# Opening in written order with two value heads together, spectra a value block later, key weights' low halves by adding transfer

## The chip, the cores and the metric

One core of a Trainium2 chip (trn2) runs one launch of the kernel. The metric is the device time of that launch in microseconds (us); lower is better. Engines are named as in the profile: PE (matmuls), PEld (its weight loads), DVE (VectorE), ACT (ScalarE), POOL (GpSimd), SP (the queue from which most transfers are issued).

## What is computed

One layer of a diffusion backbone over 512 latent tokens of width 1024, with 256 context tokens beside them, all in float32. Cut to what matters here:

```python
mod = silu(c) @ w_ada + b_ada          # six vectors of 1024: sh1, sc1, g1, sh2, sc2, g2; the same for c_ctx
hc = rmsnorm(ctx, norm1_g) * (1 + csc1) + csh1
h = rmsnorm(x, norm1_g) * (1 + sc1) + sh1
k, v, gates = h @ w_in[:, :Q_OFF]      # keys, values of four heads, gates; of hc too
q, o, hy, gm, gh = h @ w_in[:, Q_OFF:] # queries, output gate, three Hyena streams, merge gates
y = gm * (mlstm(q, k, v, gates) * o @ w_pm) + gh * (hyena(hy, spectra) @ w_ph)
x = x + g1 * (y @ w_out)
x = x + g2 * swiglu(rmsnorm(x, norm2_g) * (1 + sc2) + sh2)
return rmsnorm(x, final_g)
```

The Hyena spectra come from a small network of three sine layers, a product with its last weights, a decay window and a Fourier transform.

## The kernel before

**Products.** Tokens lie along the columns, features along the 128 partitions, in eight tiles of 128 (KT = 8). A product in float32 accuracy is made of three matmuls (mm3, L234 to L236): every operand is split into a high half rounded to the matmul's type and a low half, and high times high, high times low and low times high are added up. A split (L215, L216) is an ACT copy for the high half and a DVE subtraction for the low one. wsplit loads 512 KB of weights into a tile "wr" and splits them into "wh" and "wl"; each of the three tags has four buffers. gemm runs one output tile: 24 matmuls of 512 columns (or 256 for the context). Those that finish a group are noted in a list, and behind() queues work behind the last noted one on PE.

**Order.** The code is traced once, and a scheduler orders each engine's instructions by priority, which falls in the order written, and by readiness. high_priority(600) lets a block go earlier, issue_after(x) keeps a block behind x. Transfers are issued from SP in the order of that queue, stores from POOL.

**The opening** (from L1032). SP issues: the packed vectors (vecs, 190 KB), a small bias (bgb, 8 KB), the filter network's input (net, 386 KB), the input xT in four pieces of 512 KB, constant matrices (mats, 320 KB), 16 pieces of 256 KB of the modulation's weights for features 0 to 511 (ada_load, L329), and ahead of the last four of those one query weight (512 KB); then the first spectrum's vectors and weights, three query weights, the Fourier tables (dftf, 640 KB), the modulation's other 16 pieces, the context (1 MB). ACT squares the eight input tiles and DVE adds them (sq_sums, L403, L404), PE sums over the partitions (L407), POOL raises to the power -1/2 (L392), PE broadcasts the row to a bank (L394), DVE multiplies four input tiles (L1082). Between these run the stages of the filter network (filter_network, L420 and L423 on PE, L426 to L431 on DVE, a sine on ACT, L433) and ada_first: 32 products (64 matmul records) of 32 columns (L338), an ACT copy (L344), two transposes (L347), four DVE adds and the scale (L354, L355). modulate makes the high half of an input tile on ACT (L1113), the full value on DVE (L1118) and the low half on DVE (L1119), for tiles 0 to 3 once the first half of the modulation is there and for tiles 4 to 7 after the second (modulated). part(i, p) runs half of query tile i, four input tiles, as mm3 in the order of the tiles; the four query tiles stay in four banks. The first spectrum's steps (filter_spectrum: four products L464 and L465 with the window multiplied in on DVE, L466; sums and differences L468 to L470; a split; then 36 matmuls, three ACT copies and four DVE instructions, L503 to L508, and a store) are interleaved with these, all three steps of it.

**After the opening.** v_head (L661 to L673) makes one head's values: six blocks of 128 tokens, four of the latents and two of the context; for head 0 with the gates, one block to a bank (272 columns), for the others two (256 columns); 144 matmuls a head. The loop over the four heads runs v_head, a late query tile (q_late), and next_spectrum, which closes the open spectrum (its 36 matmuls) behind the last noted matmul and opens the next (its eight products and the split). Then eight key tiles (k_tile) run, each one gemm for 512 and one for 256 columns with convolution and SiLU on ACT and DVE and two stores on POOL; after every second one next_spectrum, and at the first of these the gates' arithmetic (gate_math). Further on: the Hyena stage, the mLSTM heads, the output products and the feed-forward layer, which the change leaves alone. There, weight_sums already has an adding transfer from POOL (L1649).

## Time and profile before

| | us |
|---|---|
| three runs, lowest, median, highest | 1200.3, 1203.37, 1204.35 |
| the profiled execution | 1201.67 |
| its span, first to last instruction | 1199.9 |

The profile is of one execution of its own. Engine times are busy times within the span; a row of a timeline gives start, length, engine, line, operation, tile written and tiles read, the count of instructions merged, and in brackets the idle time before it with what ended it.

### The profile page before, as it was taken

What the parts mean: (1) busy time and instruction counts of PE and PEld (TensorE: products, weight loads), DVE (VectorE), ACT (ScalarE), POOL (GpSimd) and SP (SyncE); (2) the same over time, 40 slices, a digit from 0 to 9 for tenths busy, and PEclk for the clock granted to TensorE, in tenths of its full rate; (3) what the DMA queues carried; (4) which work ended last, traced back from release to release, by engine and by line L of the source; (5) the groups of instructions that cost most, each with busy time, mean ns of one, the idle gap of its engine ahead of it and who ended that gap; (6) DMA issues with size and microseconds to landing.
All of it is one profiled execution on the core that took longest, in us unless ns stands there. A gap on an engine that the chain in (4) does not pass through costs nothing.

```text
span 1199.9 us, 18671 instructions
## 1 busy us (share of the span) xinstructions
PE 1166.0 (97%) x7136; PEld 1032.7 (86%) x7136; DVE 936.9 (78%) x1507; ACT 569.1 (47%) x887; POOL 113.8 (9%) x193
## 2 busy tenths in 40 slices
PE   4999999999999999999999999999999999999997
PEld 2799988988888888888788888779999999998886
DVE  5967798987989999899647887685878999896332
ACT  3763465754554455444756543233444544462221
POOL 0011110110000010101131131000101111100000
PEclk9899999999999999999999999999999999999998
DMA  9745443454245342434685586794447777757312
GB/s 346 257 144 175 144 163 117 143 206 142 100 140 184 115 155 91 173 112 137 215 249 177 181 255 220 259 310 160 136 136 185 185 185 181 189 185 250 97 49 70
DMA packets 74217, 207.50 MB, mean 173 GB/s; under 512 B 9736, under 2 KB 13584, under 8 KB 71568
## 3 DMA queue, kind: packets, MB, share of 16 engines
q1 hardware_dynamic: 56720, 154.92, 39.2%
q0 software_dynamic: 17408, 51.39, 14.4%
q8 instruction: 56, 0.92, 0.3%
q14 instruction: 33, 0.27, 0.1%
HBM read 170.62 MB, written 35.65 MB: 172 GB/s over the span
## 4 chain that ended last, share of the span: by engine, by line
PE 87%; DVE 6%; DMA 3%; ACT 2%; issue 1%; POOL 0%; SPq 0%; DVEq 0%; POOLq 0%; ACTq 0%
PE bank L234 25%; PE bank L235 25%; PE bank L236 25%; PE bank L1558 2%; PE bank L661 2%; PE bank L662 2%; PE bank L663 2%; DMA wr<-in_wph 1%; DMA wr<-in_wada 1%; DVE wl L216 1%; PE bank L617 1%; PE bank L464 1%; PE bank L465 1%; DMA ul<-in_xT 1%; PE bank L338 0%
## 5 line engine op out<-in xcount | busy, mean ns | idle before, releaser
L215 ACT ACTIVATE wh<-wr 128x1024 fp32r<-128x1024 f32 (+2 forms) x185 | 190.8, 1033 | 331.2 <-PE bank L235 226.1
L234 PE MATMUL bank<-hTh,wh 128*128 128x512 f32 (+1 forms) x896 | 326.8, 365 | 2.0 <-ACT hTh L1113 2.0
L235 PE MATMUL bank<-hTl,wh 128*128 128x512 f32 (+1 forms) x896 | 325.9, 364 | 1.9 <-DVE hTl L1119 1.9
L236 PE MATMUL bank<-hTh,wl 128*128 128x512 f32 (+1 forms) x896 | 325.4, 363 | 0.0
L216 DVE TENSOR_TENSOR wl<-wr,wh 128x1024 fp32r<-128x1024 f32 (+2 forms) x185 | 219.5, 1190 | 100.7 <-ACT wh L215 99.3
L234 PEld LDWEIGHTS bank<-hTh,wh 128*128 128x128 f32 x896 | 169.9, 190 | 27.0 <-ACT hTh L1113 2.2
L235 PEld LDWEIGHTS bank<-hTl,wh 128*128 128x128 f32 x896 | 169.7, 189 | 26.6 <-DVE hTl L1119 2.4
L236 PEld LDWEIGHTS bank<-hTh,wl 128*128 128x128 f32 x896 | 169.6, 189 | 25.5
L235 PE MATMUL bank<-big,wh 128*128 128x256 f32 (+1 forms) x346 | 110.7, 320 | 1.1 <-DVE big L216 1.1
L234 PE MATMUL bank<-big,wh 128*128 128x256 f32 (+1 forms) x346 | 110.9, 320 | 0.5 <-ACT big L215 0.5
L236 PE MATMUL bank<-big,wl 128*128 128x256 f32 (+1 forms) x346 | 110.5, 319 | 0.0
L235 PEld LDWEIGHTS bank<-big,wh 128*128 128x128 f32 x346 | 65.9, 190 | 6.4 <-DVE big L216 1.8
L234 PEld LDWEIGHTS bank<-big,wh 128*128 128x128 f32 x346 | 65.9, 190 | 5.6 <-ACT big L215 1.0
L236 PEld LDWEIGHTS bank<-big,wl 128*128 128x128 f32 x346 | 65.9, 190 | 4.5
L234 PE MATMUL bank<-uh,wh 128*128 128x256 f32 (+1 forms) x196 | 60.1, 307 | 0.0
L235 PE MATMUL bank<-ul,wh 128*128 128x256 f32 (+1 forms) x196 | 60.1, 307 | 0.0
L236 PE MATMUL bank<-uh,wl 128*128 128x256 f32 (+1 forms) x196 | 60.1, 307 | 0.0
L373 DVE SCALAR_TENSOR_TENSOR wr<-wr,crow 128x1024 f32<-128x1024 f32 x32 | 38.7, 1220 | 24.9 <-DMA wr<-in_wada 24.8
L215 ACT ACTIVATE hb<-hb 128x512 fp32r<-128x512 f32 (+1 forms) x49 | 36.5, 767 | 33.0 <-DVE hb L469 18.2
L216 DVE TENSOR_TENSOR hb<-hb,hb 128x512 fp32r<-128x512 f32 (+1 forms) x49 | 40.5, 860 | 2.0 <-ACT hb L215 1.8
L235 PEld LDWEIGHTS bank<-ul,wh 128*128 128x128 f32 x196 | 37.4, 191 | 1.7
L234 PEld LDWEIGHTS bank<-uh,wh 128*128 128x128 f32 x196 | 37.4, 191 | 1.7
(408 smaller groups left out, 2478.2 us busy)
## 6 DMA issues: line engine op xcount, KB each, us to landing
wr<-in_win SPq DMA_DIRECT2D x64, 512.0 KB, 3.7
wr<-in_w SPq DMA_DIRECT2D x42, 512.0 KB, 3.7
wr<-in_wada SPq DMA_DIRECT2D x32, 512.0 KB, 4.5
wr<-in_w SPq DMA_DIRECT2D x36, 256.0 KB
wr<-in_w POOLq DMA_DIRECT2D x18, 512.0 KB, 6.9
Kd<-K POOLq DMA_DIRECT2D x8, 1024.0 KB, 4.5
K<-Kd SPq DMA_DIRECT2D x8, 1024.0 KB, 6.5
s<-in_w SPq DMA_DIRECT2D x18, 256.0 KB, 4.4
```

The source lines that it names most:

```text
L215: act.activation(hi, x, AF.Copy)
L216: dve.tensor_sub(lo, x, hi.bitcast(F32))
L234: pe.matmul(o, wh, xh, start=first, stop=False)
L235: pe.matmul(o, wh, xl, start=False, stop=False)
L236: return pe.matmul(o, wl, xh, start=False, stop=last)
L373: dve.scalar_tensor_tensor(w, w, 1.0, crow[:], op0=ALU.mult, op1=ALU.mult, accum_out=s)
L464: pe.matmul(ps[:], lhs, w4h, start=True, stop=False)
L465: pe.matmul(ps[:], lhs, w4l, start=False, stop=True)
L661: pe.matmul(o, xh, wh, start=bool(k == 0), stop=False)
L662: pe.matmul(o, xh, wl, start=False, stop=False)
L663: m = pe.matmul(o, xl, wh, start=False, stop=bool(k == KT - 1))
L1558: m = pe.matmul(ps, w[:, k], half(h2[x][k], hf), start=n == 1, stop=n == 3 * KT)
```

## The change

The parts up to the end of the query tiles are now written instruction by instruction, and in_order() ties each engine, SP's queue among them, to that order. SP issues the input first, with vecs behind its third piece; then mats, the first modulation half, all four query weights, net, the second modulation half, the context, the first spectrum's vectors and weights, the tables. The filter network's three stages stand later: the first after the high and low halves of input tiles 0 to 3, the second within the second modulation half, the third between blocks of the value heads. Two of the four first high halves are made on DVE. The query tiles' matmuls are grouped by halves: all that read high halves of the input first. Heads 0 and 1 have their blocks interleaved and the context's normalisation spread between them; the first spectrum is opened there, not closed. In head 2 a spectrum is closed and the next opened after block 0 and after block 2, and once more after the head. Key tiles 2 to 7 get the low half of their weights in another way: ACT writes the negated high half into "wl", and a transfer from POOL adds the weights to it. The diff, cut to its core:

```diff
-    NQ, XA, AH, AQ, W0 = 4, (False, False), (2, 2), 2, (3, 0)
+    NQ = 4
...
+    @contextmanager
+    def in_order():
+        traced = nc.cur_bb.bb.instructions
+        n, last, ends = len(traced), {}, []
+        yield ends
+        for i in traced[n:]:
+            if i.engine in last:
+                tc.add_manual_dep(
+                    i, last[i.engine], mybir.DependencyInfo(mybir.DependencyClass.NoSync, mybir.DependencyReason.DATA), reason="in_order"
+                )
+            last[i.engine] = i.name
+        ends.extend(i for i in traced[n:] if i.name in last.values())
...
+    def wsplit_added(src, shape):
+        n = int(np.prod(shape[1:]))
+        raw = T(PW, [128, WMAX], F32, "wr")[:, :n]
+        hi, lo = (T(PW, [128, WMAX], F32R, t, 4)[:, :n] for t in ("wh", "wl"))
+        flat = src.rearrange("p a b -> p (a b)")
+        with tc.high_priority(PR[0]):
+            dma(raw, flat)
+            act.activation(hi, raw, AF.Copy)
+            act.activation(lo, hi.bitcast(F32), AF.Copy, scale=-1.0)
+            gp.dma_start(lo, flat.bitcast(F32R), accum_op=ALU.add)
+        return [t.rearrange("p (a b) -> p a b", a=shape[1]) for t in (hi, lo)]
...
     def v_weights(h):
-        w = 272 if h == 0 else 256
-        parts = []
-        for kh in range(2):
-            src = [(I["wv"][h, kh], slice(0, 256))]
-            if h == 0:
-                src.append((I["wg"][kh], slice(256, 272)))
-            parts.append(wsplit(src, [128, 4, w]))
-        return parts
-
-    def v_head(p, h, parts):
-        w = 272 if h == 0 else 256
+        with tc.high_priority(PR[0]):
+            return v_split(v_load(h), h)
...
+    def v_head(p, h, bvb, parts):
...
+            yield
...
+            yield
...
-        wh, wl = wsplit(I["win"][ft], [128, KT, 128])
+        wh, wl = (wsplit_added if ft > 1 else wsplit)(I["win"][ft], [128, KT, 128])
...
-    xt, cxt = [], []
-    network = filter_network(PH, net)
-    next(network)
-    sums = bank()
-    ax_, ac_ = T(PH, [128, 512], F32, "s2"), T(PH, [128, 512], F32, "s2")
-    for q in range(4):
-        t = T(PH, [128, 2, SEQ], F32, ("uh", "ul")[q % 2])
-        dma(t[:], I["xT"][:, 2 * q : 2 * q + 2])
-        for j in range(2):
-            xt.append(t[:, j])
-    dma(mats[:], I["mats"])
...
-    raws.extend(T(PW, [128, WMAX], F32, "wr") for _ in range(NQ))
-    slots = [ada_slots(PH, i) for i in range(2)]
-    units = [ada_load(PH, 0, slots[0])]
-    ada = ada_first(PH, 0, units[0], "s2")
...
+    def modulate(x, hi, lo, k, i, hi_dve=False):
+        a_, b_ = amod[:, k, i : i + 1], modT[:, 0, k, i : i + 1]
+        if hi_dve:
+            dve.tensor_scalar(hi, x, a_, b_, op0=ALU.mult, op1=ALU.add)
+        else:
+            act.activation(hi, x, AF.Identity, bias=b_, scale=a_)
+        yield
+        t = T(PH, [128, 512], F32, "s2")[:, : x.shape[-1]]
+        dve.tensor_scalar(t, x, a_, b_, op0=ALU.mult, op1=ALU.add)
+        dve.tensor_sub(lo, t, hi.bitcast(F32))
+        yield
...
+    def early_hi(i, ks):
+        if len(early) <= i:
+            early.append([v[:, :1024].rearrange("p (a b) -> p a b", a=KT) for v in (T(PW, [128, WMAX], F32R, t, 4) for t in ("wh", "wl"))])
+        act.activation(early[i][0][:, ks], raws[i][:, ks], AF.Copy)
+    def early_lo(i, ks):
+        dve.tensor_sub(early[i][1][:, ks], raws[i][:, ks], early[i][0][:, ks].bitcast(F32))
+    def early_q(i, ks, w, x):
+        for k in ks:
+            count[i] += 1
+            m = pe.matmul(qps[i][:], early[i][w][:, k], hT[x][k][:], start=count[i] == 1, stop=count[i] == 3 * KT)
+        if count[i] == 3 * KT:
+            tails.append(m.ins)
+            act.activation(qb[i], qps[i][:], AF.Identity, bias=bin_[:, FT_Q + i : FT_Q + i + 1])
 
     def ahead(n):
         for _ in range(n):
-            m = next(ada)
-        return m
-
-    for k in range(KT):
-        sq_sums(ax_, xt[k], k, 4, PH, "s2", sums)
-    next(network)
-    ahead(AH[0])
-    xb = bank()
-    rms_bcast(sums[:, :4], 4, xb, PH, "s2")
-    next(network)
-    ahead(AH[1])
-    for k in range(4):
+            next(ada)
...
+    def norm(k):
         dve.tensor_tensor(xt[k], xt[k], xb[:], op=ALU.mult)
-    early = []
-
...
+    xt, cxt = [], []
+    A, B = slice(0, 4), slice(4, KT)
+    KA, KB = range(4), range(4, KT)
+    with in_order() as ends:
+        for q in range(4):
+            t = T(PH, [128, 2, SEQ], F32, ("uh", "ul")[q % 2])
+            dma(t[:], I["xT"][:, 2 * q : 2 * q + 2])
+            for j in range(2):
+                xt.append(t[:, j])
+            if q == 2:
+                dma(vecs[:], I["vecs"])
+        dma(mats[:], I["mats"])
+        raws = [T(PW, [128, WMAX], F32, "wr")[:, :1024].rearrange("p (a b) -> p a b", a=KT) for _ in range(NQ)]
+        slots = [ada_slots(PH, i) for i in range(2)]
+        units = [ada_load(PH, 0, slots[0])]
+        for i in range(NQ):
+            dma(raws[i], I["win"][FT_Q + i])
+        dma(net[:, :772], I["net"])
+        units.append(ada_load(PH, 1, slots[1]))
+        t = T(PH, [128, KT, CTX], F32, "K")
+        dma(t[:], I["cxT"])
+        for k in range(KT):
+            cxt.append(t[:, k])
+        raw0 = T(PH, [128, 2048], F32, "hb")
+        fr, w4r = raw0[:, :1280].rearrange("p (a b) -> p a b", a=10), raw0[:, 1280:1792]
+        dec, skip = spectrum_vectors(PH, *sp[0])
+        dma(w4r, I["hw4"][sp[0]].rearrange("p f n -> p (f n)"))
+        dma(fr, I["dftf"])
+        dve.memset(silc[:], 0.0)
+        sums, xb = bank(), None
+        ax_, ac_ = T(PH, [128, 512], F32, "s2"), T(PH, [128, 512], F32, "s2")
+        for k in range(6):
+            sq_sums(ax_, xt[k], k, 4, PH, "s2", sums)
+        ada_prepare(PH)
+        ada = ada_first(PH, 0, units[0], "s2")
+        ahead(2)
+        for k in (6, 7):
+            sq_sums(ax_, xt[k], k, 4, PH, "s2", sums)
+        ahead(2)
+        bias_prepare(PH)
+        xb = bank()
+        rms_bcast(sums[:, :4], 4, xb, PH, "s2")
+        for k in KA:
+            norm(k)
+        ahead(4)
+        qps = [bank(psG) for _ in range(NQ)]
+        ms = [modulated(k, k > 1) for k in KA]
+        early_hi(0, A)
+        for k in (2, 3, 0, 1):
+            next(ms[k])
+        early_hi(1, A)
+        early_lo(0, A)
+        next(ms[0])
+        early_lo(1, A)
+        next(ms[1])
+        early_q(0, (2, 0, 3, 1), 0, 0)
+        early_q(0, KA, 1, 0)
+        early_q(1, KA, 0, 0)
+        early_q(1, KA, 1, 0)
+        early_hi(2, A)
+        early_lo(2, A)
+        next(ms[2])
+        early_hi(3, A)
+        early_lo(3, A)
+        next(ms[3])
+        network = filter_network(PH, net)
+        next(network)
+        early_q(2, KA, 0, 0)
+        early_q(2, KA, 1, 0)
+        ada = ada_first(PH, 1, units[1], "s2")
+        ahead(1)
+        early_q(3, KA, 0, 0)
+        early_q(3, KA, 1, 0)
+        ahead(2)
+        for k in KB:
+            norm(k)
+        for i in (0, 1):
+            early_hi(i, B)
+            early_lo(i, B)
+        early_q(0, KA, 0, 1)
+        ahead(1)
+        next(network)
+        early_q(1, KA, 0, 1)
+        ahead(4)
+        early_q(2, KA, 0, 1)
+        early_q(3, KA, 0, 1)
+        qb = [T(PH, [128, 512], F32, "cx2")[:] for _ in range(2)]
+        g = T(PH, [128, 2, 512], F32, "gx1", 1)
+        qb += [g[:, 0], g[:, 1]]
+        ms = [modulated(k) for k in KB]
+        for m in ms:
+            next(m)
+        for m in ms:
+            next(m)
+        for i in (2, 3):
+            early_hi(i, B)
+            early_lo(i, B)
+    opened = ExitStack()
+    for i in ends:
+        opened.enter_context(tc.issue_after(i))
+    with in_order():
+        for i in (0, 1):
+            if i:
+                csums, cb_ = bank(), bank()
+                for k in range(KT - 1):
+                    sq_sums(ac_, cxt[k], k, 2, PH, "s2", csums)
+            for k in KB:
+                for j in (2 * i, 2 * i + 1):
+                    early_q(j, (k,), 0, 0)
+                    early_q(j, (k,), 1, 0)
+            for j in (2 * i, 2 * i + 1):
+                early_q(j, KB, 0, 1)
+            if i == 0:
+                dma(bgb[:], I["bg"].broadcast_to([128, 16]))
+                v0 = v_head(PH, 0, v_bias(PH, 0), v_weights(0))
+                raws1, bias1 = v_load(1), v_bias(PH, 1)
...
+        parts1 = v_split(raws1, 1)
+        next(v0)
+        next(v0)
+        sq_sums(ac_, cxt[KT - 1], KT - 1, 2, PH, "s2", None)
+        next(v0)
+        column_sums(ac_, 2, csums)
+        next(v0)
+        next(v0)
+        rms_bcast(csums[:, :2], 2, cb_, PH, "s2")
+        next(v0)
+        raws2 = v_load(2)
+        bias2 = v_bias(PH, 2)
+        context(3)
+        next(v0)
+        context(1)
+        next(v0)
+        v1 = v_head(PH, 1, bias1, parts1)
+        context(4)
+        next(v1)
+        context(1)
+        next(network)
+        next(v1)
+        next(v1)
+        next(v1)
         stack = next(network)
         act.activation(dec[:], dec[:], AF.Abs)
         w4s = T(PH, [128, 2, 512], F32R, "hb")
         split(w4s[:, 0], w4s[:, 1], w4r)
-        list(early_split(2))
-        for k in range(4, KT):
...
+        next(v0)
+        next(v0)
+        next(v0)
+        next(v0)
+        parts2 = v_split(raws2, 2)
+        open_spectrum = [spectrum(*sp.pop(0), (dec, skip, (w4s[:, 0], w4s[:, 1])))]
+        next(open_spectrum[0])
+        marked = list(nc.cur_bb.bb.instructions)
+        next(v1)
+        next(v1)
         split(fh[:], fl[:], fr)
-    high, low = modulated(1)
-    qb = [T(PH, [128, 512], F32, "cx2")[:] for _ in range(2)]
...
+        next(open_spectrum[0])
+    opened.close()
+    for e in {i.engine for i in marked if i.engine in (nc.vector.engine, nc.scalar.engine)}:
+        opened.enter_context(tc.issue_after([i for i in marked if i.engine == e][-1]))
...
             next(open_spectrum[0])
 
-    for h in range(NH):
-        v_head(PH, h, v_weights(h))
-        PR[0] = 600
-        if h:
-            q_late(PH, h - 1)
-        next_spectrum()
+    PR[0] = 600
+    opened.close()
+    for h in range(2, NH):
+        v = v_head(PH, h, bias2, parts2) if h == 2 else v_head(PH, h, v_bias(PH, h), v_weights(h))
+        for i in range(6):
+            next(v)
+            if h == 2 and i in (1,4):
+                next_spectrum()
+        for i in range(2) if h == 2 else (h - 1,):
+            q_late(PH, i)
+        next_spectrum() if h == 2 else next_spectrum()
...
-        if ft % 2 == 0:
+        if ft in (0, 2, 4, 6):
```

## Rows read from the trace of the kernel before

**Rows 1.** the page, part 1: busy time, share, instructions of each engine.

```profile
PE 1166.0 (97%) x7136; PEld 1032.7 (86%) x7136; DVE 936.9 (78%) x1507; ACT 569.1 (47%) x887; POOL 113.8 (9%) x193
```

**Rows 2.** busy time by stretches; columns PE, PEld, DVE, ACT, POOL, clock, DMA.

```profile
0.00:100.00 100.00, 81.16 (x563) 67.89 (x564) 73.39 (x142) 54.63 (x86) 6.57 (x16) 0.97 0.67 238
180.00:200.00 20.00, 18.80 (x124) 15.40 (x123) 14.36 (x62) 10.26 (x22) 1.92 (x4) 1.00 0.35 118
900.00:1000.00 100.00, 100.00 (x835) 100.00 (x835) 90.79 (x124) 47.94 (x64) 11.88 (x10) 1.00 0.72 184
```

**Rows 3.** timeline of PE in the opening.

```profile
18.46 1.94 PE L338 MATMUL bank<-hTh,silc 128*32 128x256 f32 x16
...
22.91 1.13 PE L423 MATMUL bank<-hb,hb 128*128 128x256 f32 x4
...
24.66 2.10 PE L338 MATMUL bank<-K,silc 128*32 128x256 f32 x31
27.32 0.44 PE L347 MATMUL bank<-mats,s 128*128 128x128 f32 x2 [0.56 <-ACT s L344]
29.74 0.80 PE L234 MATMUL bank<-hTh,wh 128*128 128x512 f32 x1 [1.98 <-ACT hTh L1113]
32.45 0.79 PE L235 MATMUL bank<-hTl,wh 128*128 128x512 f32 x1 [1.92 <-DVE hTl L1119]
```

**Rows 4.** the chain that ended last, 0 to 70 us: start, time, what.

```profile
35.38 0.43 PE bank L235
...
36.91 0.23 PE bank L234
...
44.29 3.59 PE bank L338 x64
```

**Rows 5.** transfers, 0 to 40 us, GB/s in 40 equal slices.

```profile
GB/s 0 32 186 56 305 335 295 385 418 418 407 396 410 379 393 387 391 389 381 404 393 397 387 377 400 414 414 397 441 384 383 387 391 385 387 381 391 387 387 385
```

**Rows 6.** timeline of SP's queue in the opening.

```profile
16.48 2.36 SPq L329 DMA_DIRECT2D K<-in_wada  x4
```

**Rows 7.** timeline of DVE in the opening.

```profile
28.27 0.36 DVE L354 TENSOR_TENSOR modT<-bank,vecs 128x4 f32<-128x4 f32 x4
28.67 0.17 DVE L355 SCALAR_TENSOR_TENSOR amod<-modT,vecs 128x8 f32<-128x8 f32 x1
...
31.72 2.49 DVE L1119 TENSOR_TENSOR hTl<-s,hTh 128x512 fp32r<-128x512 f32 x4
```

**Rows 8.** DVE groups by form, 36 to 265 us: busy, mean ns, idle.

```profile
L216 DVE TENSOR_TENSOR wl<-wr,wh 128x1024 fp32r<-128x1024 f32 x19 | 23.1, 1222 | 12.2 <-ACT wh L215 12.1
L466 DVE TENSOR_TENSOR hb<-bank,hb 128x512 f32<-128x512 f32 x32 | 20.7, 684 | 1.5 <-PE bank L465 1.2
L216 DVE TENSOR_TENSOR hb<-hb,hb 128x1024 fp32r<-128x1024 f32 x16 | 19.3, 1218 | 1.9 <-ACT hb L215 1.8
L468 DVE TENSOR_TENSOR hb<-hb 128x1024 f32<-128x1024 f32 x8 | 9.8, 1222 | 0.1
```

**Rows 9.** the adding transfer of the feed-forward layer, L1649: min, median, max.

```profile
L1649 POOL DMA_DIRECT2D wr<-in_w x18: 1179/1189/1262, 864.4 to 1041.1; - x18
...
DMA to landing us min/median/max: 5.4/6.9/8.0
```

**Rows 10.** timeline of all engines, 205 to 215 us.

```profile
205.32 1.06 ACT L215 ACTIVATE wh<-wr 128x1024 fp32r<-128x1024 f32 x1 [1.16 <-PE bank L235]
...
206.65 1.22 DVE L216 TENSOR_TENSOR wl<-wr,wh 128x1024 fp32r<-128x1024 f32 x1
...
214.22 0.39 PE L234 MATMUL bank<-hTh,wh 128*128 128x512 f32 x1
```

**Rows 11.** timeline of PE in the key tiles.

```profile
166.85 0.39 PE L234 MATMUL bank<-hTh,wh 128*128 128x512 f32 x1
167.19 0.73 PE L234 MATMUL bank<-hb,dfh 128*128 128x256 f32 x4
```

**Rows 12.** timeline of PE, first matmul of the value heads.

```profile
67.31 0.28 PE L661 MATMUL bank<-wh,hTh 128*128 128x272 f32 x1
```

More of the change, by code (lines that the diff above doesn't have):

```diff
@@ L324, in ada_load @@
             for a in range(2):
-                if half == 0 and (kp, a) == W0:
-                    dma(raws[0][:, :1024].rearrange("p (a b) -> p a b", a=KT), I["win"][FT_Q])
                 u = slots.pop(0)
@@ L404, in sq_sums, with column_sums @@
             dve.tensor_add(acc[:, :n], acc[:, :n], sq[:, :n])
-        if k == KT - 1:
-            for b in range(nblk):
-                pe.matmul(ps[:, b : b + 1], acc[:, 128 * b : 128 * b + 128], ones[:, 0:1], start=True, stop=True)
+        if k == KT - 1 and ps is not None:
+            column_sums(acc, nblk, ps)
+    def column_sums(acc, nblk, ps):
+        for b in range(nblk):
+            pe.matmul(ps[:, b : b + 1], acc[:, 128 * b : 128 * b + 128], ones[:, 0:1], start=True, stop=True)
     def filter_network(p, net):
@@ L1029, in build @@
           ("dih", [128, 1024]), ("dil", [128, 1024]), ("cx2", [128, 512]))
-    ada_prepare(PH)
     net = T(PH, [128, 2048], F32, "hb")
-    dma(net[:, :772], I["net"])
+    silc = T(PH, [128, KT, 32], F32, "silc")
     fh = T(PH, [128, 10, 128], F32R, "dfh", 1)
@@ L1094, in build @@
-    e0 = early_split(0)
-    with tc.issue_after(next(e0)):
-        tr, am, copy = ahead(8 - AH[0] - AH[1])
-    with tc.issue_after(am):
-        list(e0)
-    dec, skip = spectrum_vectors(PH, *sp[0])
-    dma(w4r, I["hw4"][sp[0]].rearrange("p f n -> p (f n)"))
-    for i in range(1, NQ):
-        dma(raws[i][:, :1024].rearrange("p (a b) -> p a b", a=KT), I["win"][FT_Q + i])
-    dma(fr, I["dftf"])
-    units.append(ada_load(PH, 1, slots[1]))
-    t = T(PH, [128, KT, CTX], F32, "K")
-    dma(t[:], I["cxT"])
@@ L1107, in build @@
-    for k in range(KT):
-        cxt.append(t[:, k])
-    hT = ([], [])
-    def modulate(x, hi, lo, k, i, on_act):
-        a_, b_ = amod[:, k, i : i + 1], modT[:, 0, k, i : i + 1]
-        high = act.activation(hi, x, AF.Identity, bias=b_, scale=a_).ins
-        t = x if on_act else T(PH, [128, 512], F32, "s2")[:, : x.shape[-1]]
-        if on_act:
-            act.activation(t, x, AF.Identity, bias=b_, scale=a_)
-        else:
-            dve.tensor_scalar(t, x, a_, b_, op0=ALU.mult, op1=ALU.add)
-        return high, dve.tensor_sub(lo, t, hi.bitcast(F32)).ins
@@ L1121, in modulated @@
-    def modulated(p):
-        for k in range(4 * p, 4 * p + 4):
-            for i, t in enumerate(("hTh", "hTl")):
-                hT[i].append(T(PT, [128, SEQ], F32R, t))
-            low = modulate(xt[k], hT[0][k][:], hT[1][k][:], k, 0, XA[p])
-        return low
-    def part(i, p):
-        gemm(qps[i], *early[i], *hT, SEQ, range(4 * p, 4 * p + 4))
-        if p:
-            act.activation(qb[i], qps[i][:], AF.Identity, bias=bin_[:, FT_Q + i : FT_Q + i + 1])
-    high, low = modulated(0)
@@ L1134, in build @@
-    qps = [bank(psG) for _ in range(NQ)]
-    with tc.issue_after(high), tc.issue_after(low):
-        list(early_split(1))
+            next(ada)
+    def norm(k):
+        dve.tensor_tensor(xt[k], xt[k], xb[:], op=ALU.mult)
+    xt, cxt = [], []
[95 more added lines that the diff above has]
+            early_lo(i, B)
@@ new lines, in build, with context @@
+    opened = ExitStack()
[17 more added lines that the diff above has]
+                raws1, bias1 = v_load(1), v_bias(PH, 1)
+        hch = T(PH, [128, KT, CTX], F32R, "hb")
+        hcl = T(PH, [128, KT, CTX], F32R, "hb")
+        hcT = ([hch[:, k] for k in range(KT)], [hcl[:, k] for k in range(KT)])
+        cs = []
+        def context(n):
+            for _ in range(n):
+                k = len(cs)
+                if k < KT:
+                    x, a_, b_ = cxt[k], amod[:, k, 1:2], modT[:, 0, k, 1:2]
+                    dve.tensor_tensor(x, x, cb_[:, :CTX], op=ALU.mult)
+                    act.activation(hcT[0][k], x, AF.Identity, bias=b_, scale=a_)
+                    act.activation(x, x, AF.Identity, bias=b_, scale=a_)
+                if k:
+                    dve.tensor_sub(hcT[1][k - 1], cxt[k - 1], hcT[0][k - 1].bitcast(F32))
+                cs.append(k)
+        parts1 = v_split(raws1, 1)
[22 more added lines that the diff above has]
+        next(v1)
```

90 lines of the change are left out of this document (35 added, 55 removed).

## The prediction

> **What bounds the kernel now.** I read the page's busy shares first, then PE by stretches, then PE's first 40 us instruction by instruction, then whatever PE waited for there. PE is busy 1166 of 1199.9 us [rows 1], so no change that leaves its matmuls alone can win more than the 34 us in which it isn't, plus time in which it runs at half clock. By stretches [rows 2], 18.8 us of those 34 lie in the first 100 us, 1.2 us in 180 to 200 us, and in 900 to 1000 us there is none although DVE is 91% busy. This change touches only what comes before about 265 us, so the opening is where it can win, and the stage of heads and key tiles, where PE now never waits but for those 1.2 us, is where it can lose.
>
> In the opening [rows 3] PE runs the row sums, the two filter stages, the first half of the modulation (64 matmuls of 32 columns), the broadcast, and ends the modulation at 26.76 us. Then come two transposes, one query matmul at 29.74 us, and the next at 32.45 us, which waits for a low half of the input. From 32.45 us the matmuls follow each other without a gap, at first every 0.43 us, from about 36 us on every 0.23 us [rows 4]: TensorE is granted 1.2 GHz in that stretch and 2.4 GHz after it. So PE's steady work begins at 32.45 us and its steady pace at 36 us.
>
> **The opening, step by step.** Transfers: from about 8 us the queue moves 392 GB/s without a break, and the bytes up to there are those of full rate from 4.0 us on [rows 5]. The last unit of the first modulation half is issued at about 18.5 us [rows 6]; ahead of its end stand vecs 190, bgb 8, net 386, input 2048, mats 320, modulation 4096 and one query weight 512 KB, 7560 KB or 7.74 MB, so it lands at 4.0+19.7 = 23.7 us. After the change net, bgb and the query weight stand behind it: 6654 KB, 6.81 MB, 4.0+17.4 = 21.4 us. PE's queue also loses what made it finish at 26.76 us: the filter stages no longer stand between the modulation's matmuls. The last 16 of its 64 take 0.9 us at the pace of the second half (3.59 us for 64 [rows 4]) and 1.9 us at that of the first [rows 3]; I take 1.4 and get 22.8 us.
>
> From there to the modulation's vectors it was 2.1 us (26.76 to 28.84 us [rows 3, 7]), 0.5 of it because DVE was still at the filter's arithmetic, which the change puts later. That gives 24.4 us. The four high halves are divided between ACT and DVE and the first matmuls read high halves only, so steady work begins some 0.8 us later, at 25.2 us instead of 32.45 us, where DVE needed till 31.85 us to turn out the first low half [rows 7]. That is 7.2 us earlier. PE still has to run what it had done by then: the filter's stages, 2.2 us (1.06 us for the last, two smaller ones for the same together [rows 3]), and one query matmul, 0.2. **Left: 4.8 us.**
>
> The clock: of the stretch at 1.2 GHz, 3.6 us lay under steady work and cost half of that, 1.8 us [rows 4]. After the change steady work begins earlier, and nothing in this trace says when the grant will rise. Bounds: no slow stretch (1.8 us won) and one twice as long (1.8 us lost). I take 2.5 us of cost, nearer the measured 1.8 than the double: **0.7 us lost.**
>
> The second modulation half: from its last matmul to the first high half the same 2.1 us less 0.5 and 0.8 more, 2.4 us. Before, unused query matmuls lay behind it. Now only the eight that read low halves 0 to 3 do, 1.8 us at 0.23. **0.8 us lost**, bounds 0 and 2.0: its own last unit lands at about 4.0+34.4 = 38.4 us (13184 KB), near when PE wants it. Sum of the opening: 4.8 - 0.7 - 0.8 = **3.3 us won.**
>
> Hidden, at no cost: vecs behind three input loads (used only after six squares); the value loads on SP, which wait for buffers that the splits of the query weights free some 15 us after the vectors, at 40 us, and are used behind the 96 query matmuls, past 54 us; the context's normalisation, spread over the two value heads; DVE's low halves (7 us with those of the weights, four of the input 2.49 [rows 7]), covered by 32 query matmuls that read high inputs only (7.3 us at the fast pace). Lost cover there shows as PE waits before a low half.
>
> **Spectra a value block later.** Each spectrum asks of DVE four products of 0.68, four instructions of 1.22 and small ones, 8 us, and when it is closed two of each length, 3.8 us [rows 8]. With three opened and three closed about head 2, DVE has some 35 us for them, 4 us for two query tiles and 5 us for adds and weights, against PE's 36 us of head 2 and its spectra. What makes this free is head 3, 144 matmuls of 256 columns at half the 0.23 us of 512 columns, 17 us that need only weights. The total over the stage is unchanged. I take 0; without that cover it is the rival below.
>
> **Key weights.** Six instructions of 1.22 us [rows 8] leave DVE, 7.3 us; six of 1.05 us go to ACT, six adding transfers of 1.19 us each to POOL, 3.1 MB more are moved. PE waits for none of it now, so nothing is won directly. Lateness: such transfers, which the kernel has elsewhere, land 6.9 us after issue (5.4 to 8.0) [rows 9]. The tightest tile now gets its buffer at 205.32 us, has its low half at 207.87 us and starts on PE at 214.22 us [rows 10]; by transfer it would be 205.32+1.06+1.05+6.9 = 214.3 us, and only the third matmul reads it, so it is just in time. Bounds: 1.2 us won (if a freer DVE ends the idle time of 180 to 200 us [rows 2], which lies in the gates' arithmetic) and 1.2 us lost at one tile. I take 0. POOL's stores of keys stand behind a waiting transfer, and their tiles hold six buffers; with POOL 12% busy even where DVE is at 91% [rows 2] that is no bound.
>
> There is a row for the adding transfers beside a full DVE: 18 of them held POOL 1179 to 1262 ns each [rows 9], so none was held up by a DVE instruction.
> The Trainium skill, "SBUF — State Buffer", section "SBUF: two separate sides", warns of the opposite: a DMA issued from POOL has its descriptors written there, and a DVE instruction in a 2-port mode locks POOL out meanwhile. By it each of the six could be a DVE instruction later, at most six times 1.2 us; by the row, nothing. The trace doesn't bear the rule out for the two-input instructions DVE runs here, so the sum goes by the row.
>
> **Sum.** The profiled execution took 1201.67 us; 1201.67 - 3.3 = 1198.4 us. It lies 1.7 us under the median of the runs shown (1203.37) and 0.7 under the mean of all four executions; against that mean I forecast **1199.0 us**.
>
> **Rivals.** *More is won* (0.14): the clock is already up when steady work begins and the freer DVE ends the idle time about 190 us: 1199.0 - 2.5 - 1.2 = 1195.3 us. For it: the modulation's last 31 matmuls took 2.1 us where 16 earlier ones took 1.94 [rows 3], so the clock had risen under it. Against: that grant fell once PE paused, and there is a pause here too.
> *The clock eats it* (0.20): the slow stretch lies wholly under steady work (3.6 us instead of 2.5) and the second half's gap is 2.0 us instead of 0.8: 1201.3 us, no change. For it: steady work comes sooner after the sparse start.
> *A spectrum is closed at once* (0.06), the slower side: in the text of the change the third spectrum of head 2 is closed right behind its opening. If PE's queue has that order, PE stands while DVE does 3.8 + 8 us, less 1.9 us of PE's own opening: 10 us, 1209 us. It decides from the point at which no matmul of head 3 stands between. Against it: in the key tiles PE's queue is not in written order, matmuls of a spectrum stand amid those of a tile [rows 11].
> *Low halves come late* (0.05): if the margin of the tightest tile is the margin of all six, and each comes 1.2 us late, behind POOL's queue or behind a DVE instruction that holds POOL: 1206 us. Against: the 18 transfers of [rows 9], whose time on POOL hardly varies. It is also what the page named above would make of the change.
>
> **How the numbers follow.** A measurement of this kernel can tell about 0.3%, 3.6 us, so faster means under 1199.8 us. My forecast has 0.55, its own range 1197.0 to 1201.0 us, and lies under that line in 0.72 of it: 0.40. With the first rival: faster 0.54. Slower: the third rival and half of the fourth, 0.09. The rest, 0.37, is no change. The range leaves out the last two rivals and the far end of the first: 1194.5 to 1204.0 us.
>
> **What would show it.** Right: the first modulation half ends on PE before 24 us, matmuls of 512 columns run without a gap from about 25 us, the first value head starts 3 to 4 us before its 67.3 us [rows 12] less the spectrum work put off (7 us), so near 57 us; PE's waits between 60 and 265 us stay under 3 us in all. Wrong: PE waiting for a low weight half in the key tiles, or for DVE's spectrum splits about head 2; 512-column matmuls at 0.43 us beyond 33 us; a first modulation half that ends at 26 us as before, which would mean that PE's order and not the transfers set it.

## The result, and the profile after

The changed kernel takes **1206.54 us** (median of 9 runs), the kernel before 1201.70 us beside it: a ratio of 1.0047, interval 1.0032 to 1.0061. That is 4.8 us slower, where 3.3 us less were forecast, and outside the forecast range. The profiled execution took 1206.54 us with a span of 1204.8 us. In the changed kernel the three matmuls of each product are L248 to L250 (L234 to L236 before), a weight's split is L229/L230, the adding transfer L281 to L283.

Busy time by stretches in the changed kernel (columns as in [rows 2]):

```profile
0.00:100.00 100.00, 84.77 (x595) 69.81 (x596) 64.49 (x135) 48.93 (x79) 7.07 (x16) 0.98 0.66 230
180.00:200.00 20.00, 19.34 (x143) 17.05 (x143) 14.96 (x53) 9.98 (x19) 3.35 (x6) 1.00 0.51 160
200.00:220.00 20.00, 17.16 (x86) 14.16 (x85) 16.40 (x52) 14.37 (x24) 2.93 (x5) 0.91 0.63 158
900.00:1000.00 100.00, 100.00 (x835) 100.00 (x835) 90.81 (x124) 48.74 (x64) 11.95 (x10) 1.00 0.71 183
```

PE is busy 3.6 us more in the first 100 us than in [rows 2]; the opening did win. It loses 2.8 us in 200 to 220 us, 0.6 of it a wait in the gates' arithmetic that the kernel before has too, and the granted clock there is 0.91. Between 900 and 1000 us nothing differs.

PE's timeline in the opening and at the first value head:

```profile
19.69 2.39 PE L361 MATMUL bank<-K,silc 128*32 128x256 f32 x14
22.56 0.44 PE L370 MATMUL bank<-mats,s 128*128 128x128 f32 x2 [0.47 <-ACT s L367]
24.33 1.68 PE L1124 MATMUL bank<-hTh,wh 128*128 128x512 f32 x4 [1.34 <-DVE hTh L1096]
25.80 1.91 PE L1124 MATMUL bank<-hTh,wl 128*128 128x512 f32 x4
27.51 1.47 PE L1124 MATMUL bank<-hTh,wh 128*128 128x512 f32 x4
28.82 1.07 PE L1124 MATMUL bank<-hTh,wl 128*128 128x512 f32 x4
...
41.41 0.44 PE L370 MATMUL bank<-mats,s 128*128 128x128 f32 x2 [0.50 <-ACT s L367]
41.61 2.10 PE L1124 MATMUL bank<-hTl,wh 128*128 128x512 f32 x8
...
54.49 0.28 PE L703 MATMUL bank<-wh,hTh 128*128 128x272 f32 x1
```

The first modulation half ends at 22.1 us, steady work begins at 24.33 us instead of 32.45 us [rows 3], and the value heads at 54.49 us instead of 67.31 us [rows 12], with some 8.1 us of work put off: the close and the opening of a spectrum 4.2 and 1.9, the filter's last stage 1.1 and the context's sums 0.9. 12.8 less 8.1 us leaves 4.7 us won here.

What PE waited for between 60 and 270 us, in the changed kernel (microseconds in all, times, longest):

```profile
PE bank L250 <- DMA wl<-in_win: 2.8, 2, 2.2
PE bank L449 <- ACT hb L459: 1.4, 1, 1.4
PE bank L802 <- DVE hb L801: 0.7, 1, 0.7
PE bank L842 <- DVE hb L839: 0.6, 1, 0.6
PE bank L249 <- DVE hb L230: 0.6, 2, 0.5
```

and in the kernel before, which has no more than the gates' two:

```profile
PE bank L798 <- DVE hb L795: 0.6, 1, 0.6
PE bank L758 <- DVE hb L757: 0.6, 1, 0.6
```

Three waits are new: for an adding transfer (L250), for the filter's second sine (L449), and for the splits of the first spectrum (L249). The first is the longest. The timelines of ACT, POOL and PE around it:

```profile
207.44 1.06 ACT L281 ACTIVATE wh<-wr 128x1024 fp32r<-128x1024 f32 x1 [0.85 <-PE bank L490]
208.53 1.06 ACT L282 ACTIVATE wl<-wh 128x1024 fp32r<-128x1024 f32 x1
...
209.89 0.89 POOL L283 DMA_DIRECT2D wl<-in_win  x1 [3.97 <-ACT rhl L229]
...
212.39 0.40 PE L248 MATMUL bank<-hTh,wh 128*128 128x512 f32 x1
212.62 0.40 PE L249 MATMUL bank<-hTl,wh 128*128 128x512 f32 x1
212.86 0.28 PE L248 MATMUL bank<-hb,wh 128*128 128x256 f32 x1
215.37 0.50 PE L250 MATMUL bank<-hTh,wl 128*128 128x512 f32 x1 [2.24 <-DMA wl<-in_win]
...
216.66 0.63 PE L248 MATMUL bank<-hTh,wh 128*128 128x512 f32 x1
217.09 0.63 PE L249 MATMUL bank<-hTl,wh 128*128 128x512 f32 x1
```

ACT gets tile 5's buffer at 207.44 us, as the last product of a spectrum has read it, makes both copies, POOL issues at 209.89 us, and the half is there some 5.4 us later. PE had begun the tile at 212.39 us, ran three matmuls and then stood for 2.2 us, until 215.37 us. From 216.24 to 219.22 us the matmuls then follow each other every 0.43 us instead of 0.23: 1.4 us more for seven, at 1.2 GHz. The six transfers landed after 5.4 to 9.0 us:

```profile
DMA to landing us min/median/max: 5.4/5.7/9.0
```

### The profile page after: what moved, and what is told of

It is laid out like the page before. It is cut to its first block, busy times and chain, and to the rows that moved or that the text cites. A ratio compares the mean times of both kernels' runs of the same rounds, so it can differ in the third digit from the quotient of the medians.

```text
span 1204.8 us, 18689 instructions
## 1 busy us (share of the span) xinstructions
PE 1169.7 (97%) x7136; PEld 1034.5 (86%) x7136; DVE 934.1 (78%) x1507; ACT 575.7 (48%) x895; POOL 119.5 (10%) x199
## 4 chain that ended last, share of the span: by engine, by line
PE 83%; issue 5%; DMA 5%; DVE 4%; ACT 2%; POOL 1%; SPq 0%; DVEq 0%; POOLq 0%; ACTq 0%
PE bank L248 24%; PE bank L249 24%; PE bank L250 24%; PE bank L1124 2%; PE bank L1705 2%; PE bank L703 1%; PE bank L705 1%; PE bank L704 1%; DMA wr<-in_wada 1%; DMA wl<-in_win 1%; DMA wr<-in_wph 1%; PE bank L643 1%; DMA mats<-in_mats 1%; DVE wl L230 1%; DMA wr<-in_wout 1%
## 5 line engine op out<-in xcount | busy, mean ns | idle before, releaser
L229 ACT ACTIVATE wh<-wr 128x1024 fp32r<-128x1024 f32 (+3 forms) x179 | 184.5, 1033 | 304.8 <-PE bank L249 221.7
L250 PE MATMUL bank<-hTh,wl 128*128 128x512 f32 (+1 forms) x864 | 313.2, 363 | 2.8 <-DMA wl<-in_win 2.8
L248 PE MATMUL bank<-hTh,wh 128*128 128x512 f32 (+1 forms) x864 | 314.2, 364 | 0.0
L249 PE MATMUL bank<-hTl,wh 128*128 128x512 f32 (+1 forms) x864 | 313.0, 362 | 0.0
L230 DVE TENSOR_TENSOR wl<-wr,wh 128x1024 fp32r<-128x1024 f32 (+3 forms) x179 | 212.4, 1190 | 84.6 <-ACT wh L229 83.4
L250 PEld LDWEIGHTS bank<-hTh,wl 128*128 128x128 f32 x864 | 163.5, 189 | 27.7 <-DMA wl<-in_win 3.6
L248 PEld LDWEIGHTS bank<-hTh,wh 128*128 128x128 f32 x864 | 163.9, 190 | 23.0
L249 PEld LDWEIGHTS bank<-hTl,wh 128*128 128x128 f32 x864 | 163.8, 190 | 23.1
L249 PE MATMUL bank<-big,wh 128*128 128x256 f32 (+1 forms) x346 | 110.7, 320 | 1.1 <-DVE big L230 1.1
L248 PE MATMUL bank<-big,wh 128*128 128x256 f32 (+1 forms) x346 | 111.0, 321 | 0.6 <-ACT big L229 0.6
L250 PE MATMUL bank<-big,wl 128*128 128x256 f32 (+1 forms) x346 | 110.4, 319 | 0.0
L249 PEld LDWEIGHTS bank<-big,wh 128*128 128x128 f32 x346 | 65.9, 190 | 6.3 <-DVE big L230 1.8
L248 PEld LDWEIGHTS bank<-big,wh 128*128 128x128 f32 x346 | 65.9, 190 | 5.9 <-ACT big L229 1.3
L250 PEld LDWEIGHTS bank<-big,wl 128*128 128x128 f32 x346 | 65.9, 190 | 4.6
L248 PE MATMUL bank<-uh,wh 128*128 128x256 f32 (+1 forms) x196 | 60.1, 307 | 0.0
L249 PE MATMUL bank<-ul,wh 128*128 128x256 f32 (+1 forms) x196 | 60.1, 307 | 0.0
L250 PE MATMUL bank<-uh,wl 128*128 128x256 f32 (+1 forms) x196 | 60.1, 307 | 0.0
L229 ACT ACTIVATE hb<-hb 128x512 fp32r<-128x512 f32 (+1 forms) x49 | 36.1, 767 | 22.5 <-DVE hb L577 10.4
L230 DVE TENSOR_TENSOR hb<-hb,hb 128x512 fp32r<-128x512 f32 (+1 forms) x49 | 40.2, 861 | 0.2 <-ACT hb L229 0.2
L248 PEld LDWEIGHTS bank<-uh,wh 128*128 128x128 f32 x196 | 37.4, 191 | 1.7
L250 PEld LDWEIGHTS bank<-uh,wl 128*128 128x128 f32 x196 | 37.4, 191 | 1.7
```

The lines of the kernel that those rows point to most:

```text
L229: act.activation(hi, x, AF.Copy)
L230: dve.tensor_sub(lo, x, hi.bitcast(F32))
L248: pe.matmul(o, wh, xh, start=first, stop=False)
L249: pe.matmul(o, wh, xl, start=False, stop=False)
L250: return pe.matmul(o, wl, xh, start=False, stop=last)
```

## The experiments

Each was timed beside the kernel before on the same chip; the ratio is to that. A difference between two experiments compares medians that can come from different chips; where their intervals overlap, the times alone don't tell it, and the text goes to the traces.

**The adding transfers: undone, and alone.** First the changed kernel with all key tiles split on DVE:

```diff
-        wh, wl = (wsplit_added if ft > 1 else wsplit)(I["win"][ft], [128, KT, 128])
+        wh, wl = wsplit(I["win"][ft], [128, KT, 128])
```

> The changed kernel with the key tiles' low halves made by DVE again (the adding transfers undone). Theory: the adding transfers cost all of the loss in 200 to 220 us, 2.8 us of waits of PE for a low half and 1.5 to 2.4 us of half clock behind the longer one; without them 4 to 5 us come back, 1201.5 to 1202.5 us, no wait of PE for a transfer, no half clock after 40 us. Rival: the wait only moves, because the crowded spectra leave DVE late with these low halves too; then 1205 to 1207 us, with PE waiting for DVE in 200 to 220 us.

Measured: 1201.57 us, 1.0008 (0.9999 to 1.0017). So 5.0 us of the changed kernel hang on the transfers, and without them the half clock in the key tiles is gone too. Of this 4.4 us show in the traces between the first value head and a matmul behind the key tiles (54.49 to 282.29 us in the changed kernel, 54.02 to 277.40 us here): 2.8 of waits, 1.4 of half clock, 0.2 more. DVE is hardly late in their place, in the same stretch of the waits:

```profile
PE bank L449 <- ACT hb L459: 1.4, 1, 1.4
PE bank L249 <- DVE hb L230: 0.6, 2, 0.5
PE bank L842 <- DVE hb L839: 0.5, 1, 0.5
PE bank L248 <- ACT wh L229: 0.3, 1, 0.3
PE bank L250 <- DVE wl L230: 0.3, 1, 0.3
```

Then the kernel before with the transfers and nothing else of the change (the same line, the other way round):

> The kernel before with the adding transfers alone (key tiles 2 to 7). Theory that the transfers are late by themselves: PE waits for a low half at one or two tiles, 1 to 3 us, with or without a fall of the clock, 1203 to 1207 us. Rival that they are late only because the crowded spectra delay ACT and POOL in the changed kernel: no wait for a low half, 1200.5 to 1202 us.

Measured: 1200.87 us, 1.0000 (0.9991 to 1.0009), with one wait:

```profile
PE bank L236 <- DMA wl<-in_win: 1.0, 1, 1.0
```

Neither expectation holds whole: PE does wait once, but the clock doesn't fall behind that wait and the time doesn't rise. The transfers cost 5.0 us in the one kernel and nothing in the other.

**Which of the six.** At the tiles where PE waited, 5 and 7, DVE makes the low half again:

```diff
+        wh, wl = (wsplit_added if ft in (2, 3, 4, 6) else wsplit)(I["win"][ft], [128, KT, 128])
```

> The changed kernel with the adding transfer kept for key tiles 2, 3, 4 and 6 and taken back for 5 and 7, the two at which PE waited for one. Theory that only the distance in PE's queue matters, from the last matmul that reads the buffer's old contents to the tile that needs the new ones (4.9 us at tile 5, where the chain of two copies, issue and landing took 7.9): no wait for a transfer, no half clock at 216 us, as good as with all six taken back, 1201 to 1202 us. Rival, that the transfers as such slow the stage (POOL's queue, the two copies on ACT): most of the 5 us stays, 1204 to 1206 us.

Measured: 1200.70 us, 1.0003 (0.9993 to 1.0012), and the waits between 60 and 270 us have no transfer among them. Four of the six transfers are free as far as these runs can tell; those of tiles 5 and 7 are the whole loss. The order of PE shows why for tile 5. In the changed kernel 9 matmuls of 512 columns and 24 of 256 stand between the spectrum's last product (ended at 207.4 us) and tile 5: 4.9 us. Where the kernel before had the transfers alone, 24 of 512 and 29 of 256 lay between (196.4 to 205.2 us), 8.9 us, and the half came 10.4 us after the release, a wait of 1.0. Tile 7 of the changed kernel is another case:

```profile
240.57 0.50 PE L250 MATMUL bank<-hTh,wl 128*128 128x512 f32 x1 [0.58 <-DMA wl<-in_win]
```

From ACT's first copy (228.00 us) to the tile (239.36 us) it had 11.4 us, but ACT ran two other instructions between its copies (the second at 230.20 us), POOL issued at 231.55 us, and this transfer took 9.0 us, the longest of the six. The other four had 12.6 us and more.

**An earlier issue.** ACT makes the negative copy first, from the raw weights:

```diff
-            act.activation(hi, raw, AF.Copy)
-            act.activation(lo, hi.bitcast(F32), AF.Copy, scale=-1.0)
+            act.activation(lo, raw, AF.Copy, scale=-1.0)
+            act.activation(hi, raw, AF.Copy)
```

> The changed kernel with all six adding transfers, but ACT makes the negative rounded copy first, straight from the raw weights, and the positive one after it, so that each transfer can be issued 1.06 us earlier; nothing else. Theory that the transfer's landing is what PE waits for: the wait at tile 5 falls from 2.2 to about 1.1 us, the one at tile 7 goes; if the clock then still falls, 1204.5 to 1205.5 us, if it doesn't, 1202.5 to 1203.5 us. Rival that POOL's queue or the rate of the transfer sets the landing: the wait stays over 2 us and the time at 1206.

Measured: 1212.80 us, 1.0102 (1.0081 to 1.0122), slower by another 6 us. The waits, and tile 5 on ACT and POOL (the negative copy is L281, the positive one L282):

```profile
PE bank L250 <- DMA wl<-in_win: 6.0, 2, 3.7
206.90 1.06 ACT L282 ACTIVATE wh<-wr 128x1024 fp32r<-128x1024 f32 x1 [0.51 <-PE bank L490]
207.87 1.04 ACT L281 ACTIVATE wl<-wr 128x1024 fp32r<-128x1024 f32 x1
209.21 0.89 POOL L283 DMA_DIRECT2D wl<-in_win  x1 [2.33 <-ACT rhl L229]
```

The edit did not do what it was for. Though the negative copy is written first, ACT ran the positive one ahead of it, and POOL issued 0.3 us after the second: 2.3 us after ACT got the buffer, against 2.45 in the changed kernel. And the half was in place only 8.1 us after the issue instead of 5.4. That an earlier issue would help is not tested by this. The longer landing agrees with the rival, but not its time of 1206 us: PE waited 3.7 and 2.3 us, and the 512-column matmuls ran at 0.43 us behind both waits. Why the landing took longer stays open; in both kernels a load of 512 KB for a later tile is issued within 1.4 us before it and the DMA engines are 90% busy and more from 210 to 214 us. The landing varies without any edit to the key tiles too: tile 5's took 6.4 us in the trace of the sine a block later and 6.7 in that of the small tiles first, both below, which wait 3.2 and 3.6 us for it.

**Where the buffers lie.** The trace of the changed kernel has matmuls of 256 columns that read the 8 KB buffers ("hb"), which start every 0.120 us instead of 0.117. The change allocates four small tiles behind these buffers, which so lie 1312 bytes lower. One experiment puts them back, the other moves them in the kernel before:

```diff
+    place(PH, ("silc", [128, 256]), ("cth", [128, 16]), ("cch", [128, 16]), ("cb2", [128, 40]))
     net = T(PH, [128, 2048], F32, "hb")
...
-    ada_prepare(PH)
     net = T(PH, [128, 2048], F32, "hb")
+    ada_prepare(PH)
```

> The changed kernel with four small tiles (1312 bytes a partition) allocated ahead of the 8 KB buffers, so that these lie at the addresses they had in the kernel before; no instruction is changed. Theory: the pace of 0.120 us of 256-column matmuls that read these buffers, against 0.117 before, comes from the address; it goes back to 0.117 for about 620 matmuls, 1.9 us, 1204 to 1205 us. Rival: the pace comes from what else runs beside them; it stays 0.120 and the time stays at 1206.5.

> The kernel before with its 8 KB buffers 1312 bytes lower, as the changed kernel has them; nothing else. Theory that the address sets the pace: 256-column matmuls from these buffers go from 0.117 to 0.120 us and the time rises by 1.9 us, to about 1203.5. Rival: nothing changes, 1201.7.

Measured: 1206.56 us, 1.0045 (1.0030 to 1.0060), and 1201.71 us, 1.0010 (1.0000 to 1.0019). The matmuls themselves followed the address both ways. Groups of 60 to 265 us, mean duration behind the comma, first the kernel before:

```profile
L236 PE MATMUL bank<-hb,dfl 128*128 128x256 f32 x96 | 26.1, 279 | 0.0
```

the kernel before with the buffers lower:

```profile
L236 PE MATMUL bank<-hb,dfl 128*128 128x256 f32 x96 | 26.5, 283 | 0.0
```

the changed kernel:

```profile
L250 PE MATMUL bank<-hb,dfl 128*128 128x256 f32 x84 | 23.1, 283 | 0.0
```

and with the buffers where they were:

```profile
L250 PE MATMUL bank<-hb,dfl 128*128 128x256 f32 x84 | 22.8, 280 | 0.0
```

So the address sets the pace, as the theory had it, but the 1.9 us of it were too many: in the traces the kernel before loses 0.8 us by the lower buffers between 97 and 278 us (the start of the same matmuls, counted from the end), and the changed kernel gains 0.8 us by the higher ones from its first value head to 201 us, ahead of the late transfers. In the times neither can be seen: the interval of the one touches 1, and the other's profiled execution waited 4.5 us for transfers instead of 2.8.

**The sine.** In the changed kernel the second sine stands on ACT behind the context's 16 instructions (each 0.6 us), and PE's third filter stage waits for it. ACT's timeline, the last two of the 16 and the sine, and PE's:

```profile
73.42 0.58 ACT L1272 ACTIVATE hb<-K,modT,amod 128x256 fp32r<-128x256 f32 x1
74.04 0.60 ACT L1273 ACTIVATE K<-K,modT,amod 128x256 f32<-128x256 f32 x1
74.55 0.40 ACT L459 ACTIVATE hb<-hb 128x256 f32<-128x256 f32 x1
```

```profile
75.00 1.13 PE L449 MATMUL bank<-hb,hb 128*128 128x256 f32 x4 [1.43 <-ACT hb L459]
```

Written ahead of them, behind the first value block:

```diff
         next(v0)
         next(v0)
+        next(network)
         sq_sums(ac_, cxt[KT - 1], KT - 1, 2, PH, "s2", None)
...
         context(1)
-        next(network)
         next(v1)
```

> The changed kernel with the filter network's second sine and third stage written right behind the first value block of head 0, ahead of the context's 16 instructions on ACT. Theory: PE's wait of 1.4 us for that sine and the 0.6 us of slower matmuls behind it come from ACT's written order, in which the sine stands behind those 16; both go, 2.0 us won, 1204.0 to 1205.0 us. Rival: the time comes back as another wait before 245 us, 1206 to 1207 us.

Measured: 1210.94 us, 1.0079 (1.0060 to 1.0098). The one wait became two, 2.3 us together:

```profile
PE bank L433 <- DVE s L427: 1.3, 1, 1.3
PE bank L449 <- ACT hb L459: 1.0, 1, 1.0
```

The stage's arithmetic now stands on DVE in front of the context's sums, for which PE waits, and behind these waits value-head matmuls of 272 columns come every 0.225 us instead of 0.125 from 65.5 us on: 1.2 GHz again. The profiled execution was the fastest of six (1205.42 us; the others 1208.8 to 1213.3 us with a mean granted clock of 0.990 to 0.994 instead of 0.995), so where the others lost more wasn't seen.

The other way, a value block more in front of the sine:

```diff
         context(1)
-        next(network)
         next(v1)
+        next(v0)
+        next(v0)
+        next(network)
...
         split(w4s[:, 0], w4s[:, 1], w4r)
-        next(v0)
-        next(v0)
         next(v0)
         next(v0)
```

> The changed kernel with a value block of head 0 (two written calls) moved in front of the filter network's second sine, so that PE has 3 us of matmuls to run while ACT is still at the context's 16 instructions; ACT's own order is unchanged. Theory: PE's 1.4 us wait for that sine and the slower matmuls behind it are cover that is missing; both go and no new wait takes their place, 2.0 us won, 1204.0 to 1205.0 us. Rival: the network's third stage comes later too and its products then wait for it before the first spectrum, 1206 to 1207 us.

Measured: 1204.35 us, 1.0031 (1.0017 to 1.0045), 2.2 us less than the change, with intervals that overlap. By the traces PE is 1.6 us ahead at 140 us, counted from the first value head, and gives it back in longer waits behind that. L449 is no longer among the waits; the one for the transfer is still there:

```profile
PE bank L250 <- DMA wl<-in_win: 3.2, 1, 3.2
PE bank L248 <- ACT hb L229: 0.7, 2, 0.6
```

**The tables.** The transform tables are split ahead of the first spectrum's opening instead of behind it:

```diff
         parts2 = v_split(raws2, 2)
+        split(fh[:], fl[:], fr)
         open_spectrum = [spectrum(*sp.pop(0), (dec, skip, (w4s[:, 0], w4s[:, 1])))]
...
         next(v1)
-        split(fh[:], fl[:], fr)
         next(open_spectrum[0])
```

> The changed kernel with the split of the transform tables written ahead of the first spectrum's opening instead of behind it, which takes 1.5 us of DVE and 1.3 us of ACT from in front of the first spectrum's own splits. Theory: PE's waits at 100 to 103 us for those splits (1.3 us with the slower matmuls beside them) go, 1205.0 to 1206.0 us. Rival: DVE is late there because of the second spectrum's opening, and the wait stays, 1206.5.

Measured: 1205.82 us, 1.0041 (1.0028 to 1.0053), 0.7 us less, which the times can't tell from the change (the intervals overlap), but the wait L249 <- L230 is gone from the list. By its trace PE loses 0.1 us in 100 to 110 us instead of 1.3.

**Together.** First all low halves on DVE, the small tiles first, the sine ahead of the context, the tables first:

> The changed kernel with all key tiles' low halves on DVE, the small tiles allocated first, the sine ahead of the context and the tables ahead of the spectrum: the opening alone without the losses found. Theory that these account for what ate the opening's gain: 1201.6 less 2.0, 1.3 and 0.5 to 0.8, so 1197 to 1198.5 us, 3 to 4 us under the kernel before. Rival that later work is bound by something else: 1200 to 1201.5 us.

Measured: 1201.10 us, 1.0001 (0.9990 to 1.0012): no gain, because the sine's edit is the bad one; the two waits of it (1.3 and 1.0 us) stand in this trace as well, and value-head matmuls at half pace behind them from 65.7 us on. Then with the sine a block later and the four transfers kept:

> The changed kernel with adding transfers for key tiles 2, 3, 4 and 6 alone, the small tiles allocated first, the sine a value block later and the tables split ahead of the first spectrum. Theory that the opening's gain is kept once the waits behind it are taken away: 1200.7 less 2.0, 1.3 and 0.5, so 1196.5 to 1198 us, 2.5 to 4 us under the kernel before. Rival that the gain is given back in any case: 1200 to 1201.5 us.

Measured: **1196.46 us, 0.9960 (0.9944 to 0.9976)**, faster than both kernels. Between 60 and 270 us PE waits for nothing but what the kernel before has too:

```profile
PE bank L802 <- DVE hb L801: 0.7, 1, 0.7
PE bank L842 <- DVE hb L839: 0.6, 1, 0.6
```

And with DVE making all low halves:

> The kernel with all four edits (small tiles first, the sine a value block later, the tables ahead of the first spectrum), but with every key tile's low half made by DVE: what the four adding transfers that were kept are worth. Theory that they are worth nothing, since PE waits for none of these DVE instructions where DVE makes them: within 1 us of the kernel with four of them, 1196 to 1198 us. Rival that they free DVE for the gates' arithmetic or for the spectra's splits: 1 to 2 us slower, 1198 to 1199 us, with more waits of PE for DVE between 170 and 220 us.

Measured: 1197.59 us, 0.9972 (0.9960 to 0.9983). The intervals overlap: the transfers are worth nothing that these runs can tell. This kernel differs from the first of the three in the place of the sine and of one value block alone; their intervals (0.9990 to 1.0012 and 0.9960 to 0.9983) don't overlap, so that the sine's edit was the bad one is shown.

The traces close the account. The same matmul behind the key tiles, in the kernel before, in the changed one, and in the last two:

```profile
278.01 0.27 PE L617 MATMUL bank<-mats,s 128*128 128x128 f32 x1
282.29 0.39 PE L643 MATMUL bank<-mats,s 128*128 128x128 f32 x2
273.97 0.39 PE L643 MATMUL bank<-mats,s 128*128 128x128 f32 x2
272.97 0.39 PE L643 MATMUL bank<-mats,s 128*128 128x128 f32 x2
```

From the first value head to it PE takes 210.7 us in the kernel before, 218.8 with the 8.1 us put off; 227.8 in the changed kernel, 9.0 us lost; and 219.2 in each of the last two, whose first value heads come at 54.81 and 53.77 us: 0.4 us lost.

## Why the prediction was wrong

**The opening: right, and undersized.** Forecast 3.3 us, measured 4.7; the first value head, forecast near 57 us, came at 54.49. The first half ended at 22.1 us (22.8 forecast) and steady work began at 24.33 us (25.2). The term for the clock, 0.7 us lost, was none: the first twelve matmuls took 1.5, 1.7 and 1.3 us for four each, against 0.9 at full pace, 1.8 us in all, as much as before. That is this execution: of the eleven traces with these instructions up to the first value head, seven have this stretch and four (low halves on DVE, sine before the context, tables first, and the last kernel) don't, and there the first value head comes at 53.8 to 54.2 us instead of 54.5 to 55.0. Of the 2.5 us by which the value head came sooner than forecast, 1.1 is the filter's last stage, which the forecast left in the opening. Behind the second modulation half PE stood 0.5 us and the eight matmuls on low halves covered the rest (0.8 forecast, where the prediction's own 2.4 less 1.8 is 0.6, a slip that decides nothing). That the gain reaches the end once nothing behind it waits is borne out by the last two runs, 4.2 and 2.6 us under the kernel before.

**Key weights: the failed step.** They were taken at 0, with at most 1.2 us lost, because the tightest tile had 8.9 us from its buffer to PE [rows 10] and the chain by transfer needed about that. The chain was right, or too long (9.0 us reckoned, 7.9 at tile 5); the lead was not. The step took it from the trace of before, though the change moves spectra among these tiles and the queue isn't in written order [rows 11]; in the changed kernel it is 4.9 us at tile 5. At tile 7 the landing took 9.0 us, outside the 5.4 to 8.0 of [rows 9]. And it priced lateness by the wait alone, where 2.8 us of waits drew 1.4 us of half clock behind them. Undone, the transfers give 5.0 us back, 4.4 of it in this stage; the rest of the difference of the medians I can't place. The prediction's sign of being wrong, PE waiting for a low weight half, came true, and PE's waits were 6.1 us where it allowed 3. The rival "low halves come late" had the place, at 0.05; that it also had the time (1206) is chance, as two tiles were late by a total of 2.8 us and not six by 1.2 each, and other losses made up the rest.

The rule of the Trainium skill that stood against the sum ("SBUF — State Buffer", "SBUF: two separate sides") doesn't show here: the six issues held POOL 860 to 924 ns, less than the 18 of [rows 9], and the transfer that PE waited for longest, tile 5's, landed in 5.4 us, the shortest of the six. Why tile 7's took 9.0 us stays open.

**The filter's stages: counted as work, not as a chain.** The opening's sum has them at 2.2 us of PE, and lists the context's normalisation as hidden. As work they were no more than that, but the second sine was written behind the 16 instructions of the context on ACT: 2.0 us lost (a wait of 1.4 and slower matmuls behind it), 1.6 given back by a block of cover in the trace, 2.2 by the medians.

**Spectra a value block later: not 0.** The cover by head 3 was argued for DVE's total; the first close came while DVE still had the tables' split in front of the spectrum's own: 1.3 us in the trace; the times can't tell it. The rival of a spectrum closed at once (10 us) did not come about.

**Not foreseen:** 0.8 us for the address of the buffers, by the traces of both kernels.

The terms as measured: 4.7 won in the opening; 5.0, 2.0, 1.3 and 0.8 lost, 9.1 in all (the traces have 9.0, with 4.4 for the transfers); 4.4 us slower, against 4.8 us by the medians.

## What to carry to other kernels

A transfer that takes over an engine's work is judged by its lead in the order of the new kernel, buffer's release to first reader, tile by tile; what matters is not whether the engine gets freer but which tile's lead is shorter than the chain at its longest (here 7.9 us at one tile and 12.5 at another), and it can be kept for the others. A wait of a few microseconds in a dense stretch of PE may cost half as much again by the clock, as the 2.8 us here did. Work that is put off joins the written order of each engine it uses, so ask of every stage what stands in front of its slowest link there, not only whether the totals fit.

## What the hardware showed that was not expected

The pace of 256-column matmuls depended on where the 8 KB buffers they read lay: 283 ns and every 0.120 us with the buffers 1312 bytes lower, 279 ns and every 0.117 us where they had been, in both kernels, with the same instructions. Why was not tried. And the granted clock fell behind one wait of 2.2 us amid dense work (behind those of 2.3 to 3.7 us in other traces too), but not behind one of 1.0 us or the sine's of 1.4. Waits no longer than these were followed by a fall where two came close together: 1.0 and 1.3 us, ending 5.5 us apart (the sine ahead of the context, 65.5 us), and 1.3 and 0.6 us, ending 1.1 us apart (the kernel of 1196.46 us, at 793 us, far behind the change).
